# A product that nobody reads behind each chain product of the first mixer, and three PSUM banks for the chain in place of four

## The chip, the cores and the metric

The kernel runs on one core of one Trainium2 chip. The metric is the device time of one launch in microseconds; the figure for a kernel is the median of its runs. A separate execution was recorded by the hardware profiler, and all rows below come from that one.

## What is computed

The reference is a block of two layers on 1024 tokens of width 1024, in float32. Each layer is a mixer and an MLP, with an RMS norm ahead of and behind each:

```python
for layer in range(2):
    u = rmsnorm(h, norm_mix_pre[layer])
    mix = hybrid_ab_mixer(u, ...) if layer == 0 else retention_mixer(u, ...)
    h = h + rmsnorm(mix, norm_mix_post[layer])
    u = rmsnorm(h, norm_mlp_pre[layer])
    f = square(relu(u @ mlp_w_up[layer])) @ mlp_w_down[layer]
    h = h + rmsnorm(f, norm_mlp_post[layer])
```

The change lies in the first mixer. It holds two recurrences over time with eight heads of 64 each: a gated delta rule (GDN) and an RWKV-7 recurrence. Both carry a state S of 64x64 per head from one stretch of tokens to the next, and both need, in each stretch, the inverse of a triangular matrix:

```python
def step(S, inp):                       # gated delta rule, per chunk
    v_new = u_c - w_c @ S               # u_c, w_c come from the triangular solve
    o = qd_c @ S + attn_c @ v_new
    S = S * bd_c + kd_c.T @ v_new
    return S, o
```

## The kernel before

**Units and stages.** The first mixer works through 16 units: two halves of 512 tokens, in each four pairs of heads, for each pair one RWKV unit and one GDN unit. A unit has three stages. Stage a (`rwkv_a`, `gdn_a`) projects the input with weights that are split in two parts, so that each projection is 24 products of 128x512 in the one-pass type float32r, and prepares keys, values and the 128x128 blocks of the triangular matrix. Stage b (`base_inverse`) inverts the 32x32 diagonal blocks on POOL (lines 621 and 625), with DMAs through DRAM ahead of it and behind it. Stage c (`rwkv_c`, `gdn_c`) first completes the inverse on TensorE (`full_inverse`: six rounds, each four plain float32 products followed by a `copy_predicated` on DVE at line 668), and then walks the chain: four chunks of 128 tokens one after the other, each a few small float32 products whose results go to ACT or DVE and back as the next product's operand.

**The chain's products.** In an RWKV chunk they are R (read by ACT, line 832), U (read by DVE, line 839), the new state (read by DVE, lines 854 and 858) and the output `py` (read by ACT, lines 866 and 868). In a GDN chunk they are the old state's part (read by DVE, line 1017), W (ACT, line 1024), the new state (DVE, lines 1035 and 1037) and the output `po` (ACT, lines 1044 and 1046). The first chunk of a sequence has no state to read and the last makes no new one.

**PSUM.** Eight banks of 128x512 float32. In this mixer banks 0 and 1 take the projections, 2 and 3 the other products of stage a, and banks 4 to 7 take everything in stage c and the transposes of the first norm. They are handed out as a ring: `bank_area(4, 5, 6, 7)` gives one bank after the other, and who takes a bank waits until its last readers are done.

**What sets the order.** `weave` interleaves the generators of the stages on a clock of its own, which counts the estimated TensorE time that the helper `mm` adds up (`spent`). At most four units are alive. The program is then ordered once more: it is built under `TileContext(nc, schedule_with_timeline_sim=True)` (line 1884), a framework that tracks which tile each instruction reads and writes, makes the semaphore waits from that, and fixes the order of each engine's queue by its own simulated timeline: of the instructions whose inputs are there it takes the one that the program has first. On the chip each queue then runs in that fixed order.

Line 345 loads `ident`, line 409 `mask3`, line 1571 a table of the second mixer; line 266 is the last step of a norm and line 272 its transposes; line 987 multiplies the matrix blocks of a GDN unit, line 312 splits inputs.

The helper `mm` calls `PE.matmul` (line 185), so most rows of TensorE bear line 185 whatever they compute. A plain float32 product stands in the trace as two records.

Of the kernel before, what the change touches and what calls it, by code (L numbers as in the profile page):

```python
# [13 lines left out]
BF16 = mybir.dt.bfloat16  # L14
# [6 lines left out]
P = 128  # L21
# [3 lines left out]
HT = 512  # L25
# [84 lines left out]
def hybrid_block_kernel(  # L110
# [20 lines left out]
    PE, ACT, DVE, POOL, SP = nc.tensor, nc.scalar, nc.vector, nc.gpsimd, nc.sync  # L131
# [3 lines left out]
    def mk(pool, shape, tag, dt=F32, **kw):  # L135
        if isinstance(pool, Area):
            return pool.take(shape, tag, dt, **kw)
        uid[0] += 1
        return pool.tile(shape, dt, tag=tag, name=f"{tag}_{uid[0]}", **kw)
# [7 lines left out]
    banks = [mk(psum, [P, HT], f"bank{i}") for i in range(8)]  # L147
# [4 lines left out]
    def bank_area(*ids):  # L152
        return Banks([banks[i] for i in ids]).area(len(ids))
# [14 lines left out]
    ident = mk(glob, [P, P], "ident")  # L168
# [15 lines left out]
    def mm(ps, lhsT, rhs, start, stop):  # L184
        PE.matmul(ps, lhsT, rhs, start=start, stop=stop)  # L185
        n = max(256, int(np.prod(rhs.shape[1:])) * (1 if rhs.dtype == F32R else 2))
        spent[0] += n / 2400 * (1 if rhs.dtype == F32R else 2)
# [87 lines left out]
    def pair(pool, name):  # L275

        return [[mk(pool, [P, 4, HT], f"{name}{n}{g}", F32R) for g in range(2)] for n in "HL"]
# [43 lines left out]
    def layer0(late, meanwhile):  # L321


        with ExitStack() as es:
            up = region((0, 32)).area()
            weight_area(40, 56)
            psj, psb, psi = bank_area(0, 1), bank_area(2, 3), bank_area(4, 5, 6, 7)
            psc = psi
            ug = pair(up, "u")
            nrm = region((156, 204)).area(2)  # L330
            xs = []
# [308 lines left out]
            def full_inverse(MT, xx, r):  # L640


                xc, TT = xx
                Xd = Xds[0]
                xt = mk(pp, [P, 8, 32], "xt", bufs=1)
                DVE.transpose(xt.rearrange("p h r -> p (h r)"), xc.rearrange("p h r -> p (h r)"))
                for i in range(4):
                    b = slice(32 * i, 32 * i + 32)
                    ACT.copy(Xd[b, :, b], xt[b])
                yield  # L650
                Pms = []
                for hd in range(2):
                    o = slice(4 * hd, 4 * hd + 4)
                    ps = mk(psi, [P, NCH, P], "cb")
                    for n in range(NCH):
                        mm(ps[:, n, :], MT[:, 4 * hd + n, :], Xd[:, 4 * hd + n, :], True, True)
                    Pm = mk(cs, [P, NCH, P], "Pm")
                    DVE.tensor_tensor(out=Pm, in0=ps, in1=blk.unsqueeze(1).to_broadcast([P, NCH, P]), op=ALU.mult)
                    Pms.append(Pm)
                    yield  # L660
                r["go"] = True
                for c in (32, 64, 96):
                    for hd in range(2):
                        o = slice(4 * hd, 4 * hd + 4)
                        ps = mk(psi, [P, NCH, P], "cb")
                        for n in range(NCH):
                            mm(ps[:, n, c:P], Pms[hd][:, n, :], TT[:, 4 * hd + n, c:P], True, True)
                        DVE.copy_predicated(
                            TT[:, o, c:P], above.bitcast(U32).unsqueeze(1).to_broadcast([P, NCH, P])[:, :, c:P], ps[:, :, c:P]
                        )  # L670
                        yield
                r["inv"] = True
# [127 lines left out]
            def rwkv_c(p, hf, r):  # L800
# [7 lines left out]
                for j in range(NCH):  # L808
                    M3 = []
                    for hd in range(2):  # L810
                        hr = slice(64 * hd, 64 * hd + 64)
                        sl = slice(j * P, j * P + P)
                        ps = mk(psi, [P, 3, P], "cb")
                        mm(ps[:, 0:2, :], Kt[hr, sl], AR[hr, j], True, True)
                        mm(ps[:, 2, :], Bt[hr, sl], AR[hr, j, 1, :], True, True)
                        M = M3s[hd]
                        DVE.copy_predicated(M, mask3.bitcast(U32), ps)
                        M3.append(M)
                        yield
                    V = r["Vc"][:, j, :]  # L820
                    first, final = hf == 0 and j == 0, hf == 1 and j == NCH - 1
                    Ssc = mk(cs, [P, P], "Ssc%d" % par, bufs=1)
                    if not (first or final):
                        ACT.activation(Ssc, S, AF.Copy, scale=r["eLC"][:, j : j + 1])
                    ps = mk(psc, [P, P], "cb")
                    if not first:
                        mm(ps, AR[:, j, 0, :], S, True, False)
                    for hd in range(2):
                        hc = slice(64 * hd, 64 * hd + 64)
                        mm(ps[:, hc], M3[hd][:, 0, :], V[:, hc], first, first or hd == 1)  # L830
                    R = mk(cs, [P, P], "R%d" % par, bufs=1)
                    ACT.copy(R, ps)
                    yield
                    ps = mk(psc, [P, P], "cb")
                    for hd in range(2):
                        hc = slice(64 * hd, 64 * hd + 64)
                        mm(ps[:, hc], TT[:, 4 * hd + j, :], R[:, hc], True, True)
                    U = mk(cs, [P, P], "U%d" % par, bufs=1)
                    DVE.tensor_tensor(
                        out=U.rearrange("p (h d) -> p h d", h=2), in0=ps.rearrange("p (h d) -> p h d", h=2),  # L840
                        in1=bc(rho[:, 1, j, :], 64), op=ALU.mult,
                    )
                    yield
                    if not final:
                        ps = mk(psc, [P, P], "cb")
                        mm(ps, KBV[:, 0, j, :], V, True, False)
                        mm(ps, KBV[:, 1, j, :], U, False, True)
                    py = mk(psc, [P, P], "cb")
                    if not first:
                        mm(py, AR[:, j, 1, :], S, True, False)  # L850
                    for hd in range(0 if final else 2):
                        hc = slice(64 * hd, 64 * hd + 64)
                        if first:
                            DVE.tensor_scalar(
                                out=S[hc, hc], in0=ps[hc, hc], scalar1=r["eLC"][hc, j : j + 1], scalar2=None, op0=ALU.mult
                            )
                            continue
                        DVE.scalar_tensor_tensor(
                            out=S[hc, hc], in0=ps[hc, hc], scalar=r["eLC"][hc, j : j + 1], in1=Ssc[hc, hc],
                            op0=ALU.mult, op1=ALU.add,  # L860
                        )
                    for hd in range(2):
                        hc = slice(64 * hd, 64 * hd + 64)
                        mm(py[:, hc], M3[hd][:, 1, :], V[:, hc], first, False)
                        mm(py[:, hc], M3[hd][:, 2, :], U[:, hc], False, first or hd == 1)
                    ACT.copy(Y[:, j, :], py)
                    for hd in range(2):
                        ACT.activation(R[:, 0:64], py[:, 64 * hd : 64 * hd + 64], AF.Square, accum_out=s[:, 2 * j + hd : 2 * j + hd + 1])
                    yield
# [130 lines left out]
            def gdn_c(p, hf, r):  # L1000
# [7 lines left out]
                for j in range(NCH):  # L1008
                    first, final = hf == 0 and j == 0, hf == 1 and j == NCH - 1
                    R = mk(cs, [P, P], "R%d" % par, bufs=1)  # L1010
                    if first:
                        rhs = r["Vt"][:, j, :]
                    else:
                        rhs = R
                        ps = mk(psc, [P, P], "cb")
                        mm(ps, r["kE"][:, j, :], S, True, True)
                        DVE.tensor_tensor(out=R, in0=r["Vt"][:, j, :], in1=ps, op=ALU.subtract)
                        yield
                    ps = mk(psc, [P, P], "cb")
                    for hd in range(2):  # L1020
                        hc = slice(64 * hd, 64 * hd + 64)
                        mm(ps[:, hc], TT[:, 4 * hd + j, :], rhs[:, hc], True, True)
                    W = mk(cs, [P, P], "U%d" % par, bufs=1)
                    ACT.copy(W, ps)
                    yield
                    if not final:
                        ps = mk(psc, [P, P], "cb")
                        mm(ps, r["Kd"][:, j, :], W, True, True)
                    po = mk(psc, [P, P], "cb")
                    if not first:  # L1030
                        mm(po, r["qE"][:, j, :], S, True, False)
# [856 lines left out]
```

## Time and profile before

| | |
|---|---|
| median of 3 runs | 3279.22 us (3261.0 to 3289.69) |
| profiled execution, its own time | 3272.72 us |
| its span, first to last instruction | 3271.0 us |
| mean granted TensorE clock | 0.952 |
| TensorE busy | 3100.0 us (95%), 16424 records |
| DVE, ACT, POOL busy | 1996.6, 1307.8, 1243.3 us |

How to read it: the busy time of TensorE (PE) includes the modelled end of its products, so back to back products overlap and the time from start to start is the span of a stretch divided by the count in it. PEclk is the share of TensorE's full clock of 2.4 GHz that was granted; 0.50 is 1.2 GHz. The first norm takes the first 26 us, the first mixer reaches from there to about 1075 us, the first MLP, the second mixer and the second MLP fill the rest.

### The profile page before, as it was taken

What the parts mean: (1) busy time and instruction counts of PE and PEld (TensorE: products, weight loads), DVE (VectorE), ACT (ScalarE), POOL (GpSimd) and SP (SyncE); (2) the same over time, 40 slices, a digit from 0 to 9 for tenths busy, and PEclk for the clock granted to TensorE, in tenths of its full rate; (3) what the DMA queues carried; (4) which work ended last, traced back from release to release, by engine and by line L of the source; (5) the groups of instructions that cost most, each with busy time, mean ns of one, the idle gap of its engine ahead of it and who ended that gap; (6) DMA issues with size and microseconds to landing.
All of it is one profiled execution on the core that took longest, in us unless ns stands there. A gap on an engine that the chain in (4) does not pass through costs nothing. (4 is left out here: it accounts for less than half of the span.)

```text
span 3271.0 us, 44331 instructions
## 1 busy us (share of the span) xinstructions
PE 3100.0 (95%) x16424; PEld 2648.7 (81%) x16424; DVE 1996.6 (61%) x3427; ACT 1307.8 (40%) x2336; POOL 1243.3 (38%) x1549
## 2 busy tenths in 40 slices
PE   8889899899999889999999999999999989999998
PEld 6678787788788668878888899998999878877886
DVE  6445446555534865557578665667655675558585
ACT  5332333332323655544345333234432355553343
POOL 1664354454350067756150111112011057657060
PEclk9898879998979889999999999999999999999999
DMA  5221222221323545585354322344222456566354
GB/s 171 68 58 47 56 72 60 61 63 41 78 77 121 193 138 184 188 293 189 111 173 162 103 78 84 91 136 135 78 84 84 125 172 208 178 244 219 99 165 142
DMA packets 395609, 411.13 MB, mean 126 GB/s; under 512 B 69120, under 2 KB 303488, under 8 KB 394880
## 3 DMA queue, kind: packets, MB, share of 16 engines
q1 hardware_dynamic: 395392, 408.29, 39.7%
q8 instruction: 129, 2.11, 0.3%
q14 instruction: 88, 0.72, 0.1%
HBM read 312.28 MB, written 95.94 MB: 125 GB/s over the span
## 5 line engine op out<-in xcount | busy, mean ns | idle before, releaser
L185 PE MATMUL bank<-piece,piece 128*128 128x512 f32 (+7 forms) x10032 | 1740.7, 335 | 66.1 <-ACT piece L312 14.1
L185 PEld LDWEIGHTS bank<-piece,piece 128*128 128x128 f32 (+1 forms) x10032 | 1501.9, 199 | 273.2 <-issue 34.6
L1184 DVE TENSOR_TENSOR piece<-piece,piece 128x512 fp32r<-128x512 f32 (+2 forms) x436 | 596.4, 1394 | 191.7 <-ACT piece L1183 188.4
L1183 ACT CAST piece<-piece 128x512 fp32r<-128x512 f32 (+2 forms) x436 | 353.7, 838 | 548.0 <-PE bank L1468 207.0
L1315 PE MATMUL bank<-piece,piece 128*128 128x512 f32 x896 | 352.2, 394 | 20.4 <-ACT piece L1183 7.7
L1468 PE MATMUL bank<-piece,piece 128*128 128x512 f32 x896 | 352.0, 394 | 13.0 <-DVE piece L1184 13.0
L1316 PE MATMUL bank<-piece,piece 128*128 128x512 f32 x896 | 351.7, 393 | 1.9 <-DVE piece L1246 1.2
L1469 PE MATMUL bank<-piece,piece 128*128 128x512 f32 x896 | 351.0, 393 | 0.2 <-DVE piece L1184 0.2
L1317 PE MATMUL bank<-piece,piece 128*128 128x512 f32 x896 | 347.8, 392 | 0.9 <-DVE piece L1184 0.9
L205 DVE TENSOR_TENSOR piece<-piece,piece 128x1024 fp32r<-128x1024 f32 x202 | 258.4, 1280 | 130.4 <-ACT piece L204 129.1
L204 ACT CAST piece<-piece 128x1024 fp32r<-128x1024 f32 x204 | 213.5, 1047 | 284.6 <-PE bank L185 263.1
L1467 PE MATMUL bank<-piece 128*128 128x512 f32 x832 | 323.4, 392 | 2.5 <-ACT piece L1183 1.9
L1431 POOL TENSOR_TENSOR piece<-piece,piece 128x1024 f32<-128x1024 f32 (+1 forms) x72 | 215.0, 3005 | 263.4 <-DMA piece<-in_mlp_w_down_dram 207.5
L1596 POOL TENSOR_TENSOR piece<-piece,piece 128x512 f32<-128x512 f32 x32 | 64.6, 2018 | 605.9 <-DVE piece L1595 439.0
L621 POOL TENSOR_TENSOR piece<-piece 128x120 f32<-128x120 f32 (+22 forms) x496 | 186.6, 376 | 233.4 <-DMA piece<-dm 178.7
L1315 PEld LDWEIGHTS bank<-piece,piece 128*128 128x128 f32 x896 | 169.8, 190 | 58.6 <-ACT piece L1183 8.3
L1468 PEld LDWEIGHTS bank<-piece,piece 128*128 128x128 f32 x896 | 169.9, 190 | 50.8 <-DVE piece L1184 15.3
L625 POOL TENSOR_TENSOR piece<-piece,piece 128x120 f32<-128x120 f32 (+22 forms) x496 | 188.4, 380 | 37.4
L1316 PEld LDWEIGHTS bank<-piece,piece 128*128 128x128 f32 x896 | 170.0, 190 | 38.4 <-DVE piece L313 1.6
L1317 PEld LDWEIGHTS bank<-piece,piece 128*128 128x128 f32 x896 | 169.9, 190 | 36.7 <-DVE piece L1184 1.6
L1469 PEld LDWEIGHTS bank<-piece,piece 128*128 128x128 f32 x896 | 170.4, 190 | 36.0 <-DVE piece L1184 0.6
L1467 PEld LDWEIGHTS bank<-piece 128*128 128x128 f32 x832 | 157.2, 189 | 36.0 <-ACT piece L1183 2.3
(243 smaller groups left out, 3045.8 us busy)
## 6 DMA issues: line engine op xcount, KB each, us to landing
hd<-piece SPq DMA_DIRECT2D x208, 256.0 KB
piece<-hd SPq DMA_DIRECT2D x104, 512.0 KB
piece<-in_ret_w_in_dram SPq DMA_DIRECT2D x96, 512.0 KB
piece<-in_mlp_w_down_dram SPq DMA_DIRECT2D x80, 512.0 KB
piece<-in_mlp_w_up_dram SPq DMA_DIRECT2D x32, 1024.0 KB
piece<-in_ab_w_in_dram SPq DMA_DIRECT2D x60, 512.0 KB
piece<-in_ret_w_out_dram SPq DMA_DIRECT2D x32, 512.0 KB
h<-piece SPq DMA_DIRECT2D x24, 512.0 KB
```

Source lines behind the costliest of these rows:

```text
L185: PE.matmul(ps, lhsT, rhs, start=start, stop=stop)
L204: ACT.copy(hi, raw)
L205: eng.tensor_tensor(out=lo, in0=raw, in1=hi, op=ALU.subtract)
L1183: ACT.copy(hi, src)
L1184: eng.tensor_tensor(out=lo, in0=src, in1=hi, op=ALU.subtract)
L1315: PE.matmul(ps, w[0][:, k, :], u[0][:, k, :], start=start and k == 0, stop=False, skip_group_check=True)
L1316: PE.matmul(ps, w[0][:, k, :], u[1][:, k, :], start=False, stop=False, skip_group_check=True)
L1317: PE.matmul(ps, w[1][:, k, :], u[0][:, k, :], start=False, stop=stop and k == 3, skip_group_check=True)
L1431: eng.tensor_tensor(out=out, in0=a, in1=b, op=op)
L1467: PE.matmul(ps, a[0], b[0], start=first, stop=False)
L1468: PE.matmul(ps, a[1], b[0], start=False, stop=False)
L1469: PE.matmul(ps, a[0], b[1], start=False, stop=last)
```

## The change

A helper `fill` is added. It issues one product of `ident` (read as bfloat16, 128 columns) with `mask3` (read as bfloat16, 512 columns) into bank 7, whole. Nobody reads it. `ident` and `mask3` are constants that are loaded once at the start. `fill()` is called behind the products of each round of the block inverse and behind the products R, U, new state (RWKV) and old state's part, W, new state (GDN) of each chunk; not behind the outputs `py` and `po`. Bank 7 is taken out of the ring, which has three banks (4, 5, 6) left. `fill` calls `PE.matmul` itself and adds nothing to `spent`, so the clock of `weave` runs as before.

```diff
-            psj, psb, psi = bank_area(0, 1), bank_area(2, 3), bank_area(4, 5, 6, 7)
+            psj, psb, psi = bank_area(0, 1), bank_area(2, 3), bank_area(4, 5, 6)
             psc = psi
+            idle = banks[7]
+
+            def fill():
+
+                PE.matmul(idle, ident.bitcast(BF16)[:, 0:P], mask3.rearrange("p a t -> p (a t)").bitcast(BF16)[:, 0:HT],
+                          start=True, stop=True)
...
                         for n in range(NCH):
                             mm(ps[:, n, c:P], Pms[hd][:, n, :], TT[:, 4 * hd + n, c:P], True, True)
+                        fill()
...
                         mm(ps[:, hc], M3[hd][:, 0, :], V[:, hc], first, first or hd == 1)
+                    fill()
                     R = mk(cs, [P, P], "R%d" % par, bufs=1)
...
                         mm(ps[:, hc], TT[:, 4 * hd + j, :], R[:, hc], True, True)
+                    fill()
...
                         mm(ps, KBV[:, 1, j, :], U, False, True)
+                        fill()
...
                         mm(ps, r["kE"][:, j, :], S, True, True)
+                        fill()
...
                         mm(ps[:, hc], TT[:, 4 * hd + j, :], rhs[:, hc], True, True)
+                    fill()
...
                         mm(ps, r["Kd"][:, j, :], W, True, True)
+                        fill()
```

## Rows read from the trace of the kernel before

**Rows 1.** Windows; columns: stretch, length, busy (count) of PE, PEld, DVE, ACT, POOL, PEclk, DMA, GB/s.

```profile
10.00:26.00 16.00, 9.16 (x39) 7.39 (x38) 15.39 (x38) 11.51 (x24) 5.70 (x2) 1.00 1.10 309
26.00:100.00 74.00, 73.88 (x363) 58.08 (x362) 41.97 (x93) 34.49 (x58) 5.26 (x6) 1.00 0.41 109
100.00:300.00 200.00, 178.23 (x970) 149.37 (x970) 107.22 (x238) 67.69 (x146) 116.94 (x278) 0.90 0.24 62
300.00:1000.00 700.00, 651.32 (x3497) 551.31 (x3496) 359.57 (x882) 219.96 (x573) 336.65 (x806) 0.87 0.24 62
```

**Rows 2.** Windows of single stretches of the first mixer, columns as in Rows 1.

```profile
309.50:313.00 3.50, 0.64 (x5) 0.20 (x3) 0.69 (x1) 0.00 (x0) 3.19 (x7) 0.96 0.00 0
313.00:336.50 23.50, 23.50 (x81) 18.92 (x82) 6.30 (x14) 3.64 (x8) 13.28 (x41) 0.50 0.04 7
336.50:353.00 16.50, 16.50 (x83) 13.39 (x83) 7.27 (x15) 6.14 (x16) 4.13 (x9) 1.00 0.27 78
425.50:466.00 40.50, 39.95 (x167) 36.20 (x168) 18.39 (x48) 9.26 (x27) 27.35 (x67) 0.50 0.16 44
```

**Rows 3.** Waits of PE from 100 to 1075 us: total us, times, longest.

```profile
PE bank L185 <- ACT piece L312: 10.2, 3, 4.8
PE bank L185 <- DVE piece L1017: 8.4, 2, 8.2
PE bank L185 <- DVE piece L987: 7.8, 5, 2.9
PE bank L185 <- POOL piece L621: 5.5, 1, 5.5
PE bank L185 <- ACT piece L1046: 2.3, 3, 1.0
PE bank L185 <- ACT piece L868: 0.5, 2, 0.2
```

**Rows 4.** Windows of dense one-pass products, at either level of the clock; columns as in Rows 1.

```profile
131.80:135.20 3.40, 3.40 (x8) 2.70 (x9) 1.67 (x5) 1.92 (x5) 2.51 (x10) 0.50 0.00 1
1300.00:1400.00 100.00, 100.00 (x443) 82.81 (x442) 57.58 (x68) 51.25 (x85) 71.77 (x49) 1.00 0.59 186
```

**Rows 5.** Timeline of DMA issues from 0 to 40 us: start, us, queue, line, what.

```profile
2.19 0.43 SPq L345 DMA_DIRECT2D ident<-in_cst_dram  x1
8.31 3.04 SPq L409 DMA_DIRECT2D piece<-in_cst_dram  x1
17.64 0.43 SPq L1571 DMA_DIRECT2D tab<-in_cst_dram  x1
```

**Rows 6.** Timeline of PE from 0 to 40 us; in brackets the idle time before and its end.

```profile
12.31 1.97 PE L272 MATMUL bank<-ident,piece 128*128 128x128 f32 x8 [0.99 <-DVE piece L266]
15.56 1.97 PE L272 MATMUL bank<-ident,piece 128*128 128x128 f32 x8 [1.28 <-DVE piece L266]
22.09 1.97 PE L272 MATMUL bank<-ident,piece 128*128 128x128 f32 x8 [4.56 <-DVE piece L266]
23.88 1.22 PE L185 MATMUL bank<-piece,piece 128*128 128x512 f32 x2
24.89 1.57 PE L272 MATMUL bank<-ident,piece 128*128 128x128 f32 x8
```

**Rows 7.** Groups of DVE and ACT by form, 100 to 1075 us: count, busy us, mean ns.

```profile
L668 DVE COPY_PREDICATED piece<-piece,bank 128x384 f32<-128x384 uint32 x32 | 18.5, 582 | 11.1 <-PE bank L185 10.9
L839 DVE TENSOR_TENSOR piece<-bank,piece 128x128 f32<-128x128 f32 x32 | 9.2, 288 | 32.6 <-PE bank L185 32.2 <-ACT piece L1046 0.3
L1017 DVE TENSOR_TENSOR piece<-piece,bank 128x128 f32<-128x128 f32 x28 | 7.9, 281 | 20.2 <-PE bank L185 19.4 <-ACT piece L832 0.7
L866 ACT COPY piece<-bank 128x128 f32<-128x128 f32 x32 | 8.2, 256 | 39.6 <-PE bank L185 38.5 <-DVE piece L858 1.1
L868 ACT ACTIVATE piece<-bank 128x64 f32<-128x64 f32 x64 | 14.5, 227 | 0.6
L868 ACT ACTIVATION_READ_ACCUMULATOR piece<-bank 128x1 f32 x64 | 13.0, 203 | 0.0
```

## The prediction

> **What bounds the kernel now.** I read the windows first, because the change touches one stage. In the first mixer TensorE is the busy engine: 178.23 of 200 us from 100 to 300, 651.32 of 700 from 300 to 1000, while DVE, ACT and POOL are each busy at most 59% of it [rows 1]. It is not at its full clock: the mean grant is 0.90 and 0.87 there. The reader is to see both losses: 21.8 + 48.7 = 70.5 us in which TensorE is idle, and (1 - 0.90) x 200 + (1 - 0.87) x 700 = 20 + 91 = 111 us of clock that was not granted. Next come single stretches, to see when the clock is low. From 309.5 to 313 TensorE is nearly idle, the grant falls, and it stays at 0.50 (1.2 GHz) for 23.5 us in which TensorE is busy throughout with the chain's small float32 products; then it is 1.00 again. From 425.5 to 466 it is the same for 40.5 us at 98.6% busy [rows 2]. [...] The waits say what ends the idle time: splits of inputs, the gated chain's DVE step, DVE line 987, POOL's block inverse [rows 3].
>
> **What a product that nobody reads costs.** The count comes from the code and agrees with the readers' rows [rows 7]: 16 units x 6 rounds = 96 (line 668 stands three times with x32, one form shown); RWKV 32 + 32 + 28, GDN 28 + 32 + 28 (lines 839 x32, 1017 x28 show the two kinds); together 276. No bfloat16 product is in the trace; the nearest is a one-pass float32r product of the same 128x512. Dense stretches give 100/443 = 0.226 us each at the full clock and 3.4/8 = 0.425 us at half [rows 4]. All 276 on TensorE's path at the full clock are **62.4 us**; all at half, 117 us. The lower end is nothing, if each falls into idle time. The Trainium skill (TensorE: Matmul & The Clock Gate, section "Back-to-back issue gap") gives N/2.4 + 2.5 ns for a bfloat16 product, 216 ns for 512 columns; by it the term would be 59.6 us.
>
> **Where they go.** This decides the sum. A fill waits for two constants and writes a bank that nobody reads, so it is ready from the landing of `mask3` on, all 276 of them. The order of a queue is not the program's: the load of a table of the second mixer (line 1571), which the program has behind the whole first layer, is issued at 17.64 us among the first mixer's loads [rows 5], and projections stand ahead of the norm's last transposes [rows 6]. What waits for nothing is put into the first place at which the framework finds nothing else ready on that engine. `mask3` is issued at 8.31 us [rows 5]. So I expect the fills in the first 300 us or so, many between the transposes and in the first projections, and few or none beside the product that they were written behind, least of all in the long stretches of low clock after 300 us. No DMA and no other queue gets an instruction.
>
> **The sum.** Full price 62.4 us. Idle time of TensorE that early fills can use: 16 - 9.16 = 6.8 us from 10 to 26 us, 0.1 from 26 to 100, 21.8 from 100 to 300 [rows 1], 28.7 in all. The framework's idle places are its own estimate and the chip's are others, and a fill that is set ahead of a waiting product runs first even if the product becomes ready; so between nothing and all of it I take half: -14. Clock: at most the 20 us not granted from 100 to 300 come back if TensorE never rests there; again half: -10. From 300 to 1000 nothing comes back. What hides the 24 us is idle and slow time that is already lost; if the fills miss it, all 62.4 are paid. 62.4 - 14 - 10 = +38.
>
> **Three banks.** Each product of stage c opens a bank; now it waits for the readers of three openings ago in place of four. Behind it on TensorE's queue stand projections and the other chain, so such a wait is idle time of the bound engine. The longest holders are the outputs: a copy and two squares with their sums, 0.256 + 2 x (0.227 + 0.203) = 1.12 us of ACT [rows 7], and there are 64 outputs (32 of each kind). Upper end: one such hold per chunk, 64 x 1.12 = 71 us. Lower end: zero or a few us below, since the framework re-sorts the queue for three banks. With four banks the waits that end on these readers are 2.3 + 0.5 us in all [rows 3]; the value is nearest to that, and I take **+5 us**.
>
> Sum: 3272.7 + 38 + 5 = **3316 us**. It is made against the profiled execution, which lies 6.5 us under the median of 3279.2; I leave that difference inside the range.
>
> **Rivals.**
> - *The fills are hidden.* All 28.7 us of early idle time taken and all 20 us of clock regained: 62.4 - 28.7 - 20 = +14, 3287 us. For it: a fill goes in where the framework sees idle time, which partly is the chip's. Against: from 26 to 100 us there is no idle time, and a place found idle by estimate is filled by many, not one.
> - *Three banks decide.* If half of the 71 us is paid, 3272.7 + 38 + 36 = 3347, and up to 3382 with all. Place: the opening of each bank in stage c; it decides once the chain's readers lag by more than one opening, as where ACT is behind with its squares. Against: the 2.8 us above. The Trainium skill (same page, section "A second HAM failure mode: psum-queue depth-cycling") says that cycling through PSUM banks makes short rests often enough that the clock swings; no run here shows how many banks that takes.
> - *The fills stay where they are written and hold the clock: faster.* Place: the long half-clock stretches, 313 to 336.5 and 425.5 to 466. If three quarters of the 111 us return (-83) and half of the 28.7 us early idle and of the 48.7 later is used (-39) against 62.4: -60, 3213 us; if only half the clock returns (-56) and no idle time is used, +6. The middle is near 3240. It wins from the point at which what the clock returns passes the 62.4 us. [...] Against: the order [rows 5, 6]. [...]
> - *The product is dropped when the program is built,* as nobody reads it. Then only the three banks are left: 3278 us. For it nothing in the trace.
>
> **How the numbers follow.** One per cent, 33 us, is about what a measurement of this kernel can tell from no change, as the runs shown span 29 us. Against the median the bounds are 3246 and 3312. The forecast (3296 to 3336) has 0.46, of which 0.28 above 3312; hidden fills 0.22; banks 0.18; clock held 0.09; dropped 0.05. Slower 0.28 + 0.18 = 0.46; within one per cent 0.18 + 0.22 + 0.05 = 0.45; faster 0.09. The range of 8 in 10 takes in the forecast, hidden fills, the dropped product and the half of the bank case up to 3356, and leaves out the clock case and the rest of the bank case: 3268 to 3356.
>
> **What the profile after would show.** A new group on TensorE at the line of `fill`, x276, and where it stands: most before 300 us proves the order, a spread to 1000 us disproves it. TensorE's records per 100 us from 26 to 300 us stay near the old number while 276 more are among them: then they are paid. The clock from 300 to 1000 stays near 0.87: right; above 0.93: the clock case. Waits of TensorE on lines 866, 868, 1044, 1046 and 668 stay under 10 us: the bank term is right; tens of us: the bank case. The prediction is wrong if the fills stand beside their products, or if the chain loses more than 30 us to banks.

## The result, and the profile after

The changed kernel takes 3332.91 us (median of 4 runs, 3329.54 to 3340.34) against 3284.45 us for the kernel before: a ratio of 1.0162 with a 95% interval of 1.013 to 1.0195, that is 43 to 64 us more. The profiled execution took 3333.58 us, its span is 3331.9 us, 60.9 more than before. The forecast was 3316 us, in a range of 3268 to 3356.

Part 1 of the page of the changed kernel: busy time, share and records of each engine.

```profile
PE 3137.3 (94%) x16683; PEld 2656.2 (80%) x16700; DVE 1996.6 (60%) x3427; ACT 1312.8 (39%) x2336; POOL 1243.5 (37%) x1549
```

TensorE has 259 more records and 37.3 us more busy time; DVE, ACT and POOL do the same work as before. First I looked for the place. The first MLP begins with one line, 1315 before and 1328 after. These are the rows of that line, with the first and last start; first the kernel before, then the changed one.

```profile
L1315 PE MATMUL bank<-piece,piece x896: 387/389/796, 1119.9 to 2935.6; 128*128 128x512 f32 x180
```

```profile
L1328 PE MATMUL bank<-piece,piece x896: 389/389/796, 1181.9 to 3000.4; 128*128 128x512 f32 x180
```

1181.9 - 1119.9 = 62.0 us: all of the loss lies ahead of the first MLP, and the rest of the kernel is unchanged. So each kernel below is read by one window, from the start to its first MLP. TensorE's busy time in it (the first number after the length) and its idle time (length less busy) make the sum. The kernel before, then the changed one:

```profile
0.00:1119.90 1119.90, 1015.02 (x5441) 853.44 (x5442) 603.61 (x1468) 393.71 (x951) 470.38 (x1113) 0.89 0.29 79
```

```profile
0.00:1181.90 1181.90, 1053.01 (x5699) 861.80 (x5717) 602.99 (x1467) 397.92 (x951) 471.62 (x1113) 0.90 0.28 75
```

Idle time went from 104.9 to 128.9 us (+24.0), busy time from 1015.0 to 1053.0 (+38.0). The products were expected to cost 62.4 us of busy time; that only 38.0 show means that other work ran faster, at a higher clock: summed over the trace's stretches at a clock of 0.50, TensorE is busy in them for 183 us up to the first MLP, against 223 us before, which is worth 20 us. The +24.0 of idle time is the surprise: 276 products that could be put into any rest, and TensorE rests more than before. (17 of the 276 have no record; at 0.22 us each, up to 4 us of what counts as idle time here is theirs.)

Where the products stand: the timeline of TensorE in the changed kernel from 0 to 30 us, which answers to [rows 6].

```profile
12.41 1.97 PE L272 MATMUL bank<-ident,piece 128*128 128x128 f32 x8 [0.98 <-DVE piece L266]
15.70 5.95 PE L333 MATMUL bank<-piece,ident 128*128 128x512 bf16 x20 [1.32 <-DMA piece<-in_cst_dram]
21.48 1.47 PE L272 MATMUL bank<-ident,piece 128*128 128x128 f32 x12
22.79 4.91 PE L333 MATMUL bank<-piece,ident 128*128 128x512 bf16 x21
```

Bursts of 20 and 21 between the transposes of the first norm, as soon as `mask3` has landed. And windows of line 333 alone (PE busy and count, PEld, PEclk of the stretch, DMA):

```profile
0.00:26.00 26.00, 9.10 (x34) 3.95 (x36) 1.00 0.97 290
26.00:300.00 274.00, 22.20 (x93) 8.98 (x100) 0.95 0.28 70
300.00:450.00 150.00, 31.81 (x133) 13.44 (x140) 0.95 0.19 46
450.00:1181.90 731.90, 0.00 (x0) 0.00 (x0) 0.87 0.27 75
```

All of them stand before 450 us, none beside the chain's work of the later units that they were written behind. The stretches of the changed kernel, columns as in [rows 1]:

```profile
10.00:26.00 16.00, 13.65 (x61) 7.87 (x61) 15.28 (x41) 11.82 (x25) 5.69 (x2) 1.00 1.10 315
26.00:100.00 74.00, 73.86 (x359) 54.37 (x361) 38.60 (x83) 32.59 (x56) 3.79 (x5) 1.00 0.36 95
100.00:300.00 200.00, 173.81 (x925) 139.00 (x930) 96.62 (x218) 60.97 (x134) 116.14 (x270) 0.93 0.26 61
300.00:450.00 150.00, 136.97 (x810) 106.31 (x815) 70.65 (x164) 42.07 (x107) 58.58 (x138) 0.95 0.19 46
450.00:1000.00 550.00, 498.73 (x2702) 423.00 (x2702) 283.62 (x713) 170.00 (x431) 249.93 (x592) 0.85 0.22 57
```

From 10 to 26 us the idle time did shrink, 6.8 to 2.4 us. The clock of 1.00 in this stretch is not a grant that the trace recorded: eight transposes take 1.97 us at 12.41 us and twelve take 1.47 us at 21.48 us, which is half and full clock. The first grant on record is at 18.7 us here and at 26.0 us in the kernel before, where eight transposes still take 1.97 us at 22.09 us [rows 6]. From 100 to 300 it grew, 21.8 to 26.2 us, although the products were there. The clock is 0.93 and 0.95 while there are products and 0.85 once they are used up; in the kernel before the same stretches have 0.90, 0.78 and 0.89. The waits of TensorE from 100 to 1130 us, which answer to [rows 3] (total us, times, longest):

```profile
PE bank L538 <- ACT piece L917: 19.9, 5, 6.0
PE bank L185 <- DVE piece L868: 16.8, 3, 8.5
...
PE bank L185 <- ACT piece L312: 6.0, 3, 4.0
...
PE bank L185 <- ACT piece L878: 3.8, 1, 3.8
...
PE bank L185 <- ACT piece L1059: 0.2, 1, 0.2
```

Lines 917, 868, 878 and 1059 are 907, 858, 868 and 1046 before. The output readers that the prediction feared (878, 1059) are waited for 4.0 us in all. New is the wait for the reader of the new RWKV state (868); that for an ACT step of the GDN preparation (917) rose from 3.2 us.

### The profile page after: what moved, and what is told of

Read it like the earlier page. It is cut to its first block, busy times and chain, and to the rows that moved or that the text cites. A ratio compares the mean times of both kernels' runs of the same rounds, so it can differ in the third digit from the quotient of the medians.

```text
span 3331.9 us, 44866 instructions
## 1 busy us (share of the span) xinstructions
PE 3137.3 (94%) x16683; PEld 2656.2 (80%) x16700; DVE 1996.6 (60%) x3427; ACT 1312.8 (39%) x2336; POOL 1243.5 (37%) x1549
## 5 line engine op out<-in xcount | busy, mean ns | idle before, releaser
L185 PE MATMUL bank<-piece,piece 128*128 128x256 f32 (+6 forms) x10032 | 1736.0, 333 | 86.1 <-DVE piece L868 16.8
L185 PEld LDWEIGHTS bank<-piece,piece 128*128 128x128 f32 x10032 | 1494.3, 198 | 292.1 <-issue 48.4
L1328 PE MATMUL bank<-piece,piece 128*128 128x512 f32 x896 | 352.2, 394 | 20.4 <-ACT piece L1196 8.3
L1328 PEld LDWEIGHTS bank<-piece,piece 128*128 128x128 f32 x896 | 169.8, 189 | 58.3 <-ACT piece L1196 8.8
L1481 PEld LDWEIGHTS bank<-piece,piece 128*128 128x128 f32 x896 | 169.5, 189 | 47.6 <-DVE piece L1197 12.3
L1329 PEld LDWEIGHTS bank<-piece,piece 128*128 128x128 f32 x896 | 170.2, 190 | 38.1 <-DVE piece L1259 1.9
L1330 PEld LDWEIGHTS bank<-piece,piece 128*128 128x128 f32 x896 | 170.1, 190 | 37.9 <-DVE piece L1197 2.3
L1482 PEld LDWEIGHTS bank<-piece,piece 128*128 128x128 f32 x896 | 169.8, 189 | 37.9 <-DVE piece L1197 2.8
```

The lines of the kernel that those rows point to most:

```text
L1328: PE.matmul(ps, w[0][:, k, :], u[0][:, k, :], start=start and k == 0, stop=False, skip_group_check=True)
L1329: PE.matmul(ps, w[0][:, k, :], u[1][:, k, :], start=False, stop=False, skip_group_check=True)
L1330: PE.matmul(ps, w[1][:, k, :], u[0][:, k, :], start=False, stop=stop and k == 3, skip_group_check=True)
L1481: PE.matmul(ps, a[1], b[0], start=False, stop=False)
L1482: PE.matmul(ps, a[0], b[1], start=False, stop=last)
```

## The experiments

All times are medians; ratios are against runs of the kernel before on the same chip (medians 3282 to 3287). "MLP" is the start of the first MLP in the profiled execution, "idle" and "busy" are TensorE's up to there. They come from one execution of each kernel, and the runs of one kernel spread by some 30 us with their mean clock (the kernel before, beside banks3: 3265.74 us at 0.957, 3297.72 us at 0.946). So a difference of 15 us in busy time shows little by itself, and the ratios decide. The profiled execution of the kernel before, 3272.7 us, lies 10 to 15 us under its medians, so differences of spans against it come out too large by about that much. In own4, 62 of the 276 products have no record: up to 13 us of its idle time is theirs.

| kernel | median us | ratio, 95% interval | MLP | idle | busy |
|---|---|---|---|---|---|
| before | 3284 | | 1119.9 | 104.9 | 1015.0 |
| changed | 3333 | 1.0162 (1.0130 to 1.0195) | 1181.9 | 128.9 | 1053.0 |
| banks3 | 3299 | 1.0058 (1.0029 to 1.0087) | 1141.5 | 134.4 | 1007.1 |
| swap3 | 3310 | 1.0078 (1.0048 to 1.0108) | 1152.2 | 132.6 | 1019.6 |
| short3 | 3298 | 1.0038 (1.0023 to 1.0054) | 1141.3 | 122.9 | 1018.4 |
| short4 | 3292 | 1.0017 (0.9999 to 1.0036) | 1125.3 | 115.6 | 1009.7 |
| front4 | 3336 | 1.0145 (1.0127 to 1.0164) | 1184.1 | 106.0 | 1078.1 |
| fill128 | 3314 | 1.0091 (1.0058 to 1.0123) | 1164.5 | 116.6 | 1047.9 |
| fill2 | 3338 | 1.0177 (1.0144 to 1.0210) | 1183.7 | 104.3 | 1079.4 |
| late | 3333 | 1.0140 (1.0113 to 1.0166) | 1176.0 | 127.6 | 1048.4 |
| held | 3299 | 1.0052 (1.0023 to 1.0082) | 1154.4 | 115.7 | 1038.7 |
| own4 | 3310 | 1.0069 (1.0050 to 1.0087) | 1149.1 | 121.6 | 1027.5 |
| held4 | 3291 | 1.0022 (0.9998 to 1.0045) | 1138.1 | 115.9 | 1022.2 |

### banks3: the banks alone

```diff
-            psj, psb, psi = bank_area(0, 1), bank_area(2, 3), bank_area(4, 5, 6, 7)
+            psj, psb, psi = bank_area(0, 1), bank_area(2, 3), bank_area(4, 5, 6)
```

> The kernel before with the ring of three banks and nothing else; no product is added, bank 7 lies idle. Theory A (the prediction's: the added products are paid at 0.226 us each, the banks cost +5): the median is within 3280 to 3295 against about 3284 before, and of the 62 us by which the first MLP starts later after the change (1119.9 to 1181.9 us) only a few us are here. Theory B (three banks decide): 3310 to 3332, the MLP starts 25 to 48 us later than before, and TensorE's waits on the chain's readers (line 1017, 1046, 868, 866, 668) together grow from 11 us by more than 20 us.

Measured 3299 us, +10 to +29 us by the interval and +20.4 from span to span (3291.4 against 3271.0): between the theories, well above +5. Its window to the first MLP:

```profile
0.00:1141.50 1141.50, 1007.10 (x5441) 843.55 (x5442) 598.49 (x1467) 397.65 (x951) 471.84 (x1113) 0.89 0.29 77
```

Idle time is up by 29.5 us, busy time down by 7.9: the banks cost rests. The clock up to the first MLP is 0.89 in both, and in the trace it falls to 0.50 there 24 times, against 23 in the kernel before. The Trainium skill (TensorE: Matmul & The Clock Gate, section "A second HAM failure mode: psum-queue depth-cycling") tells of a kernel that cycles through PSUM banks and rests so often that its clock swings; here the rests grew and the clock did not swing more. The waits of banks3, 100 to 1085 us:

```profile
PE bank L185 <- ACT piece L312: 13.5, 5, 5.4
PE bank L532 <- ACT piece L907: 13.1, 3, 5.4
PE bank L185 <- DVE piece L858: 12.9, 3, 5.9
PE bank L185 <- ACT piece L1024: 9.9, 5, 4.7
...
PE bank L185 <- ACT piece L1046: 0.2, 1, 0.2
```

The expectation's own sign for theory B looked at the wrong lines: 1046, 868 and 866 are hardly waited for. Line 858, with no wait of TensorE in the kernel before, is there three times. One of them in banks3's timeline of TensorE:

```profile
366.40 2.37 PE L185 MATMUL bank<-piece,piece 64*128 64x256 f32 x5 [4.77 <-DVE piece L858]
```

A product of 64 rows and 256 columns is the M product `mm(ps[:, 0:2, :], Kt[hr, sl], AR[hr, j], ...)` of the next chunk. Its operands have nothing to do with the state that line 858 writes; what it waits for is the bank. Counted in the order of the chain alone, with three banks the M product of the second head opens the one that the new state's product used, with four the one of U. TensorE stands still for 4.77 us with all that is queued behind. The M products of all chunks, in the kernel before and in banks3:

```profile
L185 PE MATMUL bank<-piece,piece 64*128 64x256 f32 x128 | 47.8, 461 | 0.0
```

```profile
L185 PE MATMUL bank<-piece,piece 64*128 64x256 f32 x128 | 46.2, 456 | 19.3 <-DVE piece L858 12.9 <-DVE piece L1017 6.4
```

So 19.3 of the 29.5 us of added idle time stand ahead of M products. Why the reader is so late stands in the timeline of DVE at the same place:

```profile
364.83 0.45 DVE L646 STREAM_TRANSPOSE piece<-piece 128x256 f32<-128x256 f32 x1 [12.27 <-DMA piece<-dx]
365.77 0.57 DVE L858 SCALAR_TENSOR_TENSOR piece<-bank,piece,piece 64x64 f32<-64x64 f32 x2
```

Line 646 is the first step of `full_inverse`, which takes the inverted blocks of another unit back from DRAM. DVE stood there for 12.27 us until the DMA was through, with line 858 behind it in its queue. In the changed kernel all three waits for line 868 (16.8 us) come right behind such a stand, of 15.17, 9.19 and 8.93 us.

### swap3: take that wait away

```diff
+                    py = mk(psc, [P, P], "cb")
                     if not final:
                         ps = mk(psc, [P, P], "cb")
                         mm(ps, KBV[:, 0, j, :], V, True, False)
                         mm(ps, KBV[:, 1, j, :], U, False, True)
-                    py = mk(psc, [P, P], "cb")
```

> Three banks and no added product, as in banks3, with the bank of an RWKV output opened ahead of the bank of the new state. In banks3 TensorE waits 12.9 us in three places for the reader of the new state (line 858), each time at a product whose operands have nothing to do with the state: it is the next chunk's first M product, whose bank comes three openings behind the new state's. With the swap that product's bank comes behind the U bank instead, and the new state's bank goes to the product that waits for the state anyhow. Theory F (these bank waits are what three banks cost): the waits on line 858 (here 859 or so) fall under 3 us and the median comes back to 3280 to 3292. Theory G (they are one of several places, and the new order of the queues moves others): the waits on that line go, but the median stays at 3293 to 3305.

Measured 3310 us, above the upper end of both theories and no better than banks3. The waits of TensorE in swap3, 100 to 1095 us:

```profile
PE bank L185 <- DVE piece L1017: 20.2, 5, 7.0
PE bank L532 <- ACT piece L907: 13.6, 4, 5.0
...
PE bank L185 <- ACT piece L868: 9.4, 5, 7.7
```

And the M products of swap3:

```profile
L185 PE MATMUL bank<-piece,piece 64*128 64x256 f32 x128 | 46.8, 479 | 8.7 <-ACT piece L868 8.6
```

Line 858 has gone from the list and line 868, the reader of the outputs, is new in it (9.4 us; none in banks3). 8.6 of it stand ahead of M products: in the order of the chain the swap puts the M product of the second head behind the output's bank, so the wait changed its reader. Line 1017 rose from 6.4 to 20.2, and not at the same products: in banks3 M products waited for it, here products of 128x64, the shape of the W products that need its result. This is nearest to theory G: the wait for line 858 was real and could be taken away, and others came in its place. Line 907 shows how far this reaches: it reads a bank of the pair 2 and 3, which the change leaves alone, and yet the wait for it is 3.2 us in the kernel before, 13.1 in banks3, 13.6 in swap3 and 19.9 in the changed kernel.

### short3 and short4: hold the outputs' banks for less

```diff
-                        ACT.activation(R[:, 0:64], py[:, 64 * hd : 64 * hd + 64], AF.Square, ...)
+                        ACT.activation(R[:, 0:64], Y[:, j, 64 * hd : 64 * hd + 64], AF.Square, ...)
...
-                        ACT.activation(R[:, 0:64], po[:, 64 * hd : 64 * hd + 64], AF.Square, ...)
+                        ACT.activation(R[:, 0:64], O[:, j, 64 * hd : 64 * hd + 64], AF.Square, ...)
```

> Three banks and no added product, as in banks3 (3299), with one more edit: the squares of an output are taken from its copy in SBUF and not from the bank, so that ACT holds an output's bank for one copy (0.256 us) in place of 1.12 us. Theory A (the prediction's reason: the longest holders of a bank are the outputs): the 15 us that three banks cost go away, 3280 to 3290, and the idle time of TensorE ahead of the first MLP falls from banks3's 134 us back towards 105. Theory B (the bank that is waited for is another's: the new states on DVE, the norm's and the outputs' transposes, or the new order of the queue): it stays at 3293 to 3305.

> The control to short3: four banks, no added product, the squares of the outputs taken from the copy in SBUF. Both theories: no difference from the kernel before that can be told, 3275 to 3292, as TensorE waited 2.3 + 0.5 us for these readers.

short4 (3292, at the upper end of what was expected) cannot be told from the kernel before, short3 not from banks3 (3298 and 3299): theory B, as the waits for the outputs' readers had said. Against its own control, though, three banks cost short3 6 us by the medians, where they cost banks3 15; the intervals do not tell these apart, so a part of the price may still be the holds. The M products of short3:

```profile
L185 PE MATMUL bank<-piece,piece 64*128 64x256 f32 x128 | 45.9, 451 | 0.0
```

They wait for nothing here, with three banks, and the time is that of banks3 all the same. So the M product is one place at which the price can be paid, and not the price itself.

### front4: the price of the products alone

```diff
             SP.dma_start(mask3.rearrange("p a t -> p (a t)"), cst[:, C_U : C_U + 3 * P])
+            lead = mk(psi, [P, HT], "cb")
+            for _ in range(276):
+                PE.matmul(lead, ident.bitcast(BF16)[:, 0:P], mask3...bitcast(BF16)[:, 0:HT], start=True, stop=True)
```

> The kernel before with four banks and 276 products of the same size, all in one place of the program behind the load of mask3, into one bank of the ring that is then handed on. They can't run later than the next use of that bank, so they stand in the first 100 us, where the clock is at 1.00 and TensorE hardly rests. Theory A: the price is full there, 62.4 us less at most the 6.8 us of idle time from 10 to 26 us: the first MLP starts 50 to 62 us later and the median is 3335 to 3350. Theory E (early products also give back clock or rest later on, as the second 276 of fill2 did, which added 5 us): 3290 to 3325.

Measured 3336 us, +42 to +54 by the interval; the first MLP starts 64.2 us later in the profiled execution. Its timeline of TensorE:

```profile
39.04 0.94 PE L185 MATMUL bank<-piece,piece 128*128 128x512 f32 x3
39.83 59.74 PE L412 MATMUL bank<-piece,ident 128*128 128x512 bf16 x270
99.22 1.96 PE L185 MATMUL bank<-piece,piece 128*128 128x512 f32 x7
```

One block of 276 (270 recorded), of which the last takes 0.38 us: (59.74 - 0.38) / 275 = 0.216 us from start to start, 59.6 us in all, 4% under the 0.226 us that I took from the float32r row. That is the figure that the Trainium skill gives for a single product (TensorE: Matmul & The Clock Gate, section "Back-to-back issue gap"); for a sustained stream the same section gives about 131 ns, which this block does not bear out. Idle time is 106.0 us against 104.9 and busy time 63.1 higher: in the profiled executions the products are paid in full where the clock is at 1.00 and TensorE doesn't rest. Theory A. By the ratio they cost 42 to 54 us, so a few of the 59.6 may come back later.

### fill128 and fill2: fewer columns, more products

In `fill` the 512 columns become 128, or the product is issued twice.

> The changed kernel with the added product cut from 512 to 128 columns; count, place in the program and the three banks stay. Theory A: the price goes with the columns, between 0.226/4 = 0.057 us and the 0.111 us of the smallest record in the trace before, so 276 cost 16 to 31 us in place of 62 and the time falls 31 to 46 us from the changed kernel's 3333: 3287 to 3302. Theory B (the three banks and the new order cost the most, the products little): 3318 to 3335. Both expect the products in bursts ahead of the chain, as in the changed kernel.

> The changed kernel with two added products in each place, 552 in all. Theory A: the idle and slow places that can hide any are used up by the first 276, so the second 276 cost their full price, 276 x 0.226 = 62 us: 3385 to 3400. Theory B: the price was the banks, and more products go into idle time like the first: 3333 to 3360.

fill128 took 3314 us, 19 less than the changed kernel but 12 above theory A's upper end: the columns count, yet with busy time 40.8 us over banks3 the small products gave no clock back (0.88 to the first MLP). Their own share is about 16 us (an estimate: the busy time with what was at a clock of 0.50 counted half is 16 us above banks3's); the other 25 us are the lower clock, under which TensorE is busy for 251 us against 202. Why the clock is lower is open. fill2 refutes theory A outright: the second 276 added 5 us in place of 62. Its window to the first MLP, and two stretches of it (in the changed kernel the clock is 0.86 from 450 to 900 us):

```profile
0.00:1183.70 1183.70, 1079.40 (x5993) 860.44 (x5994) 602.76 (x1468) 395.36 (x951) 474.00 (x1113) 0.94 0.27 75
300.00:450.00 150.00, 141.11 (x790) 108.00 (x789) 69.13 (x162) 40.27 (x103) 58.55 (x138) 0.93 0.18 44
450.00:900.00 450.00, 426.40 (x2465) 338.58 (x2464) 224.81 (x564) 135.57 (x338) 200.47 (x480) 0.95 0.21 56
```

Against the changed kernel, idle time fell by 24.6 us and busy time rose by 26.4 for 60 us of added work. Of the 552, 266 stand between 450 and 860 us, where there was much clock to win (0.86 to 0.95) and rests to fill. The time is in theory B's range, but only the idle half of this is theory B's reason.

### late: the same bursts at another time

```diff
             def fill(x):
+                owed[0] += 1
+                if owed[0] < 90:
+                    return
+                if owed[0] == 90:
+                    gate.append(mk(cp, [P, P // 2], "gate").bitcast(BF16))
+                    DVE.tensor_copy(gate[0], <upper halves of x>)
+                for _ in range(90 if owed[0] == 90 else 1):
+                    late_fill()        # as fill was, with gate[0] as stationary operand
```

> The changed kernel with the same 276 products of 512 columns and three banks, but the first 89 calls of fill only count; the 90th copies an operand of the chain into a small tile and issues all that are owed, and that tile is the stationary operand of every added product. So all are ready at once again, but not before some 450 us. What is tested: whether it is the place that decides what they cost. Theory E (products that stand where the clock is low give back clock, early ones don't): they stand in bursts from 450 to 900 us, the clock from there to the first MLP is above 0.92 (0.87 in the changed kernel), and the median is 3298 to 3318. Theory A (they cost their 62 us less a little, wherever they stand in bursts): 3325 to 3345.

Measured 3333 us, the time of the changed kernel: theory E falls. Its bursts stand from 471.0 to 823.5 us (90 in the first), and these are its windows:

```profile
100.00:300.00 200.00, 171.32 (x845) 142.60 (x846) 96.49 (x216) 60.37 (x133) 115.04 (x271) 0.83 0.23 58
300.00:450.00 150.00, 132.87 (x761) 113.05 (x760) 75.73 (x186) 46.89 (x116) 68.98 (x159) 0.88 0.20 50
450.00:900.00 450.00, 416.70 (x2369) 326.49 (x2369) 218.61 (x547) 137.04 (x343) 198.07 (x479) 0.94 0.22 55
```

To read them one needs the same windows of banks3, which has the same banks and no products:

```profile
100.00:300.00 200.00, 172.10 (x848) 143.25 (x847) 96.89 (x216) 60.51 (x133) 114.45 (x271) 0.83 0.23 58
300.00:450.00 150.00, 130.91 (x719) 111.45 (x718) 72.34 (x174) 46.02 (x114) 65.80 (x150) 0.85 0.20 49
450.00:900.00 450.00, 411.02 (x2313) 346.74 (x2311) 238.16 (x598) 148.51 (x379) 218.19 (x530) 0.91 0.24 61
```

Up to 300 us late is at banks3's clock (0.83), and where its bursts stand it has 0.94 for 0.91. The changed kernel has 0.93 for 0.83 and 0.95 for 0.85 where its bursts stand, but 0.86 for 0.91 behind them: what it wins early it partly loses later, for a reason that no run shows. Up to the first MLP TensorE is busy at a clock of 0.50 for 202 us in banks3, 183 in the changed kernel and 168 in late, so the bursts brought back 9 and 17 us; with one execution each, these two are not told apart.

### held, own4 and held4: the products beside the chain

In held the stationary operand is the operand of the product in front; in own4 the target is the chain's own bank ahead of its product, so that four banks can stay; held4 joins the two, behind the product, in columns of the bank that are free.

```diff
# held
-                PE.matmul(idle, ident.bitcast(BF16)[:, 0:P], mask3...
+                PE.matmul(idle, <upper halves of x>, mask3...   # x = S, R, U, W, TT[:, 4 * hd, :]
# own4
-                    ps = mk(psc, [P, P], "cb")
+                    ps = mk(psc, [P, NCH, P], "cb")
+                    fill(ps)                                  # 512 columns
+                    ps = ps[:, 0, :]
# held4
+                    pw = mk(psc, [P, NCH, P], "cb")
+                    ps = pw[:, 0, :]
...
+                    fill(R, pw[:, 1:4, :])                    # 384 columns; inverse: ps[:, :, 0:c]
```

> The changed kernel, but the added product takes its stationary operand (the upper halves of its words, read as bfloat16) from the operand that the chain's product in front of it has just used: S, R, U, W, or the inverse TT. So it can't be ready before that product is, and stands beside it. What is tested: whether the order alone (all 276 ready at the start) put the products in bursts before 450 us, and what they do where they were written. Both theories expect x276 spread from 160 to 1100 us and none before 160. Theory C (products of 512 columns beside the chain keep TensorE's clock up): mean grant from 300 to 1000 us above 0.93 instead of 0.88, the time 3225 to 3290. Theory D (the clock follows the rests, not the products): grant 0.85 to 0.90, and the price of 276 x 0.226 to 0.425 us is paid beside the chain: 3340 to 3390.

> The 276 products of 512 columns with four banks in turn: each goes into the chain's own bank ahead of the product that overwrites it, so it can't run before that bank is free and stands at most a few openings ahead of its product; no bank is taken away. Theory C (beside the chain an added product pays for itself with clock, as held against banks3 shows: 3299 against 3299): the mean grant from 300 to 1000 us is above 0.90 and the time that of the kernel before, 3275 to 3295. Theory D (in held the products were hidden in the rests that three banks made): with four banks they are paid, 3300 to 3340.

> Four banks, and the added product behind its product with an operand of it, as in held, but written into the free columns of the product's own bank: 384 columns in the chain, 128, 256 or 384 in the rounds of the inverse. Against own4 it stands behind the product and not ahead of it, so it doesn't delay it. Theory C (beside the chain the product pays for itself in clock): 3280 to 3295, the granted clock above 0.90 from 300 to 1000 us. Theory D (held was free because three banks had made rests to hide in; with four the products cost some 20 us, as in own4): 3300 to 3320.

The row of line 333 in held, with the first and last start:

```profile
L333 PE MATMUL bank<-piece,piece x276: 376/379/634, 152.4 to 1100.7; 128*128 128x512 bf16 x138
```

And its window to the first MLP:

```profile
0.00:1154.40 1154.40, 1038.72 (x5716) 857.84 (x5717) 602.56 (x1467) 397.60 (x950) 468.81 (x1113) 0.92 0.28 77
```

They stand from 152 to 1101 us: that all were ready at once is what put them in bursts. And the time is 3299 us, 34 less than the changed kernel with the same number, size and banks, and the same as banks3 without any product. Against the changed kernel idle time is 13.2 us lower and busy time 14.3. The time is near neither theory: not C (the clock from 300 to 1000 us is 0.90, not 0.93), not D (nothing is paid on balance). Record by record, 26 of the 276 last 0.59 to 0.63 us in place of 0.38, at the low clock; in the changed kernel 7 of the 259 recorded ones do, all at the start of its first burst, before the grant at 18.7 us.

With four banks own4, ahead of its product, costs 16 to 29 us (theory D by the number); held4, behind it, -1 to +15 us (theory C). That the side decides is not shown: the clock from 300 to 1000 us is 0.91 in both, above theory C's 0.90 in own4 too, and own4's products have 512 columns where held4's have at most 384, which alone makes some 15 us (an estimate from front4's row, 59.6 against up to 45). The stretch from 300 to 1000 us of held, then of held4:

```profile
300.00:1000.00 700.00, 646.74 (x3624) 536.50 (x3624) 358.25 (x882) 218.35 (x554) 329.47 (x786) 0.90 0.22 58
```

```profile
300.00:1000.00 700.00, 644.23 (x3704) 543.31 (x3701) 363.66 (x891) 221.05 (x566) 342.55 (x810) 0.91 0.23 61
```

The window of held4 to its first MLP:

```profile
0.00:1138.10 1138.10, 1022.20 (x5717) 854.60 (x5718) 603.64 (x1466) 396.98 (x950) 475.28 (x1113) 0.91 0.28 78
```

Its busy time is 7.2 us above the kernel before, although its products are worth up to 276 x 0.216 x 384/512 = 45 us (an estimate from front4's row): most of it came back as clock. Idle time is 11.0 us higher. No version here beats the kernel before.

## Why the prediction was right, and which step was not

The measured time lies in the range, 17 us above the forecast, and on the side that had the largest chance (slower by over 1%, 0.46). Some 12 of the 17 us are the base: the forecast was added to the one profiled execution at 3272.7 us, and the median is 3284.45. Against the medians the change is 48.5 us, for a forecast of 43. Against banks3, the profiled executions split the change in two: 3291.4 - 3271.0 = 20.4 us for the banks and 3331.9 - 3291.4 = 40.5 us for the products; by the ratios it is about 19 and 34.

- **Full price, 62.4 us: right within 5%.** front4 shows 0.216 us each, 59.6 in all, and that where there is neither rest nor low clock at least 42 us of it are paid, by the profiled executions all.
- **Where they go: right in kind, too early in place.** Bursts, none beside its product, and held shows that readiness is the reason. But of 259 records 127 stand before 300 us (34 + 41 + 52), not most; the last at 446 us. Perhaps the framework sees fewer free places than I assumed. It made no difference: late has them after 470 us and takes the same time.
- **Idle time used, -14, and clock regained, -10: right in sum.** Against banks3 the changed kernel has 134.4 - 128.9 = 5.5 us less idle time, and 45.9 us more busy time, 16.5 less than 62.4. Together -22 for a forecast of -24. The 16.5 are not all clock: 9 us are (183 us busy at a clock of 0.50 for 202), 3 the lower price, and 4 the 17 products without a record, which count as idle time. Put right, that is about 9 us of rests and 9 us of clock. The clock came back up to 450 us, part of it from 300 on (0.95 for 0.85), where I had allowed nothing, and some was lost again behind (0.86 for 0.91).
- **Three banks, +5: mis-sized, and the largest miss of a term.** It measures +20.4 between the profiled executions, +10 to +29 by the interval. The step that failed is "The longest holders are the outputs": with three banks TensorE waits 0.2 us for their readers. It waits where a product that could have run ahead opens the bank of a reader that is late: in banks3 19.3 us ahead of M products, in the changed kernel 16.8 us for line 868, there each time behind DVE's stand for a DMA. That these waits are the whole price is not shown, as swap3 and short3 lost them and not the time. My test for this term (under 10 us on lines 866, 868, 1044, 1046 and 668) came out at 9.0 us in the changed kernel and would have called the term right: a list of lines is a bad test where the order is made anew; idle time up to a fixed point is a good one.
- **Sum.** 62.4 - 22 + 20.4 = 60.8 on 3271.0, the span of 3331.9; as the 22 is what is left of 62.4, it has to close.
- **A row read wrongly.** In the stretch of low clock from 313 to 336.5 us TensorE is not busy throughout with the chain's small products. From 327 us on they are products of 128x512, at 0.50 up to 336.5:

```profile
327.04 11.45 PE L185 MATMUL bank<-piece,piece 128*128 128x512 f32 x36
```

The rivals: *hidden fills* would need 49 us won, 22 were. *Three banks decide* has the right term, at a little over half of its lower price of 36 us, and the wrong holders. *Dropped* is out: the records are there. *In place and faster* was priced too high: held and held4 put the products there, and beside the chain they win back about what they cost, not 60 us more. The clock from 300 to 1000 us rose from 0.87 to 0.90 and 0.91 only (0.89 in banks3), far from the full clock. The Trainium skill's statement that activity releases the throttled state (TensorE: Matmul & The Clock Gate, section "What's actually happening") has the right sign in these rows.

**Open.** Why one product behind each chain product wins more than bursts do (13.2 us of rest and 14.3 us of busy time) is measured and not explained. Whether the 20 us of three banks are all waits for banks, or in part an unlucky order of the queues, is not separated: swap3 and short3 took waits away and got others. No run was made in which DVE does not stand for the DMA.

## What to carry to other kernels

An instruction that depends on constants alone has no place: this framework put it, in bursts, far ahead of where it was written. To keep it beside other work, give it an operand of that work (3333 to 3299 us here, with only that operand changed). And before a buffer is taken out of a ring, list for each opening what it would wait for, above all the openings whose operands are ready early, and look what the reader's engine may stand for with the reader still in its queue; here the length of the holds did not give the price.

## What the runs showed that was not expected

- 552 added products cost 58 us by the ratio where 276 cost 53: from 450 to 900 us the second set found a clock of 0.86 and left it at 0.95.
- TensorE rests more in the changed kernel than before (128.9 against 104.9 us), with 276 products that wait for nothing; with 552 it is back at 104.3.
- A product written into free columns of a bank is waited for by the readers of the others: in held4 the DVE step that reads U (line 851, line 839 before) is released in 20 places by the added product, although it reads other columns. That it waits longer for that isn't shown: these waits come to 27.3 us, and in the kernel before it waited 32.2 us for U's own product.
- The chain's readers stand behind DMA waits of another unit in DVE's queue (12.27 us in the place above), and in banks3 and the changed kernel TensorE waits behind that for a bank.
